# Two hybrid layers on one core: the merge and its gates get memory beside the attention

## The chip, the core and the metric

The kernel runs on one core of one Trainium2 chip. The metric is the device time of one execution in microseconds. The engines are TensorE (PE, with its weight loads as PEld), VectorE (DVE), ScalarE (ACT), GpSimd (POOL) and SyncE (SP), which here only issues transfers. All matrix products accumulate in PSUM; operands live in SBUF.

## What is computed

A model of two layers on 512 tokens of width 1024. Each layer is a feed-forward block, a mixer and a second feed-forward block. The mixer has three branches, which are gated and summed before one output product:

```python
def hybrid_mixer(...):
    proj = h @ w_in
    ret_p, dsa_p, rwkv_p, gate_p = split_cols(proj, GROUP_SIZES)
    y_ret = retention(...)          # ends: silu(g) * o
    y_dsa = sparse_attention(...)   # top-256 keys by an index score, then softmax
    y_rwkv = rwkv7_time_mix(...)    # a recurrence over tokens
    g_ret, g_dsa, g_rwkv = jnp.split(jax.nn.sigmoid(gate_p), N_BRANCH, axis=-1)
    merged = g_ret * (y_ret @ p_ret) + g_dsa * (y_dsa @ p_dsa) + g_rwkv * (y_rwkv @ p_rwkv)
    return merged @ w_out
```

All is float32. The kernel makes each large product from three products of split operands: a value is stored as a high part (`hi`, rounded) and the remainder (`lo`), and `hi*hi + hi*lo + lo*hi` is summed.

## The kernel before

Activations are held transposed, as 8 tiles of 128 x 512. `dense` (L116) makes one 128 x 512 output block: for each of its input blocks three matmuls (`mm3`, L105, whose lines are L109, L111 and L113). Weights come in pieces of 128 x 512 (`raw`, four buffers, L53), and each piece is split by `split` (L49 on ACT for the high part, L50 on DVE for the remainder) into `whi` and `wlo` (three buffers each). The output goes to one of four PSUM tiles `psd`.

The mixer runs two streams of work. The first is the recurrence, class `Rwkv`: four pairs of heads, one after another. For a pair, `next` prepares operands (`front2`, `mid`), `chain` (L505) goes through eight chunks of 64 tokens, and `post` (L545) normalises. A chunk of the chain is four small steps on PE (L512, L522, L532, L539) with a small DVE copy or update between each two, so that PE would wait at every step. These have the highest priority ("rec").

The second stream is `other` (L922), a Python generator: the index and the retention, the attention (`attend`, L785), 32 gate products (`gates`, L858) and the merge (`merge`, L874). `fill` (L73) takes a number of matmuls from it at each step of the recurrence, by the tables FZ to FF (L224 to L230), so that large products stand between the small steps. The attention's own work after its projection (L799 to L839) is written in one piece and placed by the scheduler, which follows priorities and its own estimate of when operands are ready. The final order on each engine is fixed when the program is built.

`gates` computes first, for each of 8 blocks, the gate of the retention output: it loads the block `yret[b]` from DRAM, multiplies it and stores it to `yg[b]`. Then it computes 24 gate factors, tanh values that it stores to `thd`. `merge` loads the gated outputs, splits them into `yh0`..`yh7` and `yl0`..`yl7`, and computes per branch (8, 4 and 4 input blocks) eight output blocks, with a `th` tile loaded for each; the sums are kept in tiles `m0`..`m7`. The third branch waits until the recurrence is done. It has 8 x 3 x (8 + 4 + 4) = 384 matmuls per layer. At the end the merged sums are split (`mh`, `ml`) and multiplied with `w_out` (192 matmuls, L958), and the residual `x` is loaded back (L955) and added.

Memory decides what may overlap. Pools are stacked from two sides of SBUF, and a tile in a new pool waits for the tiles that had its addresses before. `gp` lies where the retention's pool was. `mrg` is opened after the attention's pool `dsa` is closed, and lies on its addresses:

```python
            yield from ds.attend(a["wt"][l, 4])
            with right("gp") as gp:
                yield from gates(K, l, gp, a, yd[0], yg, thd)
        with right("mrg") as mp:
            yield from merge(K, l, mp, mh, a, (yg, yd[1], yd[2]), thd, rw)
```

Of the kernel before, what the change touches and what calls it, by code (L numbers as in the profile page):

```python
# [7 lines left out]
P = 128  # L8
F32 = mybir.dt.float32
F32R = mybir.dt.float32r  # L10
# [3 lines left out]
ALU = mybir.AluOpType  # L14
T = 512
# [6 lines left out]
class Core:  # L22
    def __init__(self, tc, ctx):
        self.tc, self.nc, self.ctx = tc, tc.nc, ctx
        self.n = 0
        self.work, self.urgent, self.between = iter(()), deque(), True
        self.early = deque()
        self.level = {"rec": 0, "split": 200000, "norm": 400000, "late": 800000}
        pool = lambda n, **kw: ctx.enter_context(tc.tile_pool(name=n, bufs=1, **kw))
        self.psp = pool("psp", space=bass.MemoryType.PSUM)  # L30
        self.cp = pool("cp")
        self.wp = pool("wp")
        self.xp = pool("xp")
        self.dp = pool("dp", space=bass.MemoryType.DRAM)
# [198 lines left out]
class Rwkv:  # L233


    def __init__(self, K, pool, par, w2a2, g2, cst, y_out):
        self.K, self.nc, self.tc, self.p = K, K.nc, K.tc, pool
        self.cst, self.y_out = cst, y_out
        self.gate, self.done = None, False
        nc = self.nc  # L240
        self.par = self.t("par", [P, NPAR])
        nc.sync.dma_start(self.par, par)

        raw = self.t("tha")
        nc.sync.dma_start(raw, w2a2)
        self.wa = self.stack(raw)
        self.g2 = self.t("g2")
        nc.sync.dma_start(self.g2, g2)
        self.bones = self.t("bones", [P, P], dt=F32R)
        nc.vector.tensor_copy(self.bones, cst["bones"])  # L250
        self.omm = self.t("omm", [P, 14])
# [64 lines left out]
    def pairs(self, blk):  # L316
        K = self.K
        K.run(self.lora(blk))
        K.run(self.front(0, blk))
        self.blk = blk  # L320
        K.fill(F0)
        nxt = self.next(0)
        for p in range(4):
            d = nxt
            K.fill(FM[p])
            with K.at("rec"):
                self.chain(d)
            K.fill()
            if p < 3:
                nxt = self.next(p + 1)  # L330
            with K.at("rec"):
                self.post(d)
        self.done = True
# [515 lines left out]
def gate(K, w, tl):  # L849

    ps = yield from K.dense(w, K.xg)
    g, th = tl("g", 2), tl("th", 2)
    K.nc.vector.tensor_tensor(out=g, in0=ps, in1=K.rb, op=ALU.mult)
    K.nc.scalar.activation(th, g, AF.Tanh, scale=0.5)
    return g, th


def gates(K, l, pool, a, yret, yg, thd):  # L858

    nc = K.nc  # L860
    tl = lambda tag, bufs=1, dt=F32: pool.tile([P, T], dt, tag=tag, name=K.nm(tag), bufs=bufs)
    for b in range(8):
        x = tl("y", 2)
        nc.sync.dma_start(x, yret[b])
        g, th = yield from gate(K, a["wf"][l, 14 + b], tl)
        nc.vector.scalar_tensor_tensor(out=g, in0=th, scalar=1.0, in1=g, op0=ALU.add, op1=ALU.mult)
        nc.vector.scalar_tensor_tensor(out=x, in0=g, scalar=0.5, in1=x, op0=ALU.mult, op1=ALU.mult)
        nc.sync.dma_start(yg[b], x)
    for j, d in enumerate(thd):
        _, th = yield from gate(K, a["wf"][l, 22 + j], tl)  # L870
        nc.sync.dma_start(d, th)


def merge(K, l, pool, mh, a, yd, thd, rw):  # L874

    nc = K.nc
    tl = lambda tag, bufs=1, dt=F32: pool.tile([P, T], dt, tag=tag, name=K.nm(tag), bufs=bufs)
    mg = []
    for br, (nb, o, pw) in enumerate(((8, 0, "pret"), (4, 0, "pdsa"), (4, 4, "prw"))):
        while br == 2 and not rw.done:  # L880
            yield "wait"
        y = []
        for b in range(nb):
            x = tl("y", 2)
            nc.sync.dma_start(x, yd[br][b])
            hi, lo = tl(f"yh{o + b}", dt=F32R), tl(f"yl{o + b}", dt=F32R)
            K.split(x, hi, lo)
            y.append((hi, lo))
        for j in range(KC):
            i = 8 * br + j  # L890
            if i < len(thd):
                th = tl("th", 2)
                nc.sync.dma_start(th, thd[i])
            else:
                _, th = yield from gate(K, a["wf"][l, 22 + i], tl)
            pp = yield from K.dense(a[pw][l, j], y)
            if br == 0:
                m = tl(f"m{j}")
                mg.append(m)
                nc.vector.scalar_tensor_tensor(out=m, in0=th, scalar=1.0, in1=pp, op0=ALU.add, op1=ALU.mult)  # L900
            else:
                nc.vector.scalar_tensor_tensor(out=th, in0=th, scalar=1.0, in1=pp, op0=ALU.add, op1=ALU.mult)
                nc.gpsimd.tensor_tensor(out=mg[j], in0=mg[j], in1=th, op=ALU.add)
            if br == 2:
                K.split(mg[j], *mh(j))


def mixer(K, l, a, c, xd, xnew, out_cb, done):
    nc, tc = K.nc, K.tc
    yd = [[K.dram([P, T], f"y{br}_{b}") for b in range(nb)] for br, nb in enumerate((8, 4, 4))]  # L910
    yg = [K.dram([P, T], f"yg_{b}") for b in range(8)]
    thd = [K.dram([P, T], f"th_{b}") for b in range(NTH)]
    right = lambda n: tc.tile_pool(name=K.nm(n), bufs=1, side="right", reuse_waits="tile")

    def y_dsa(qt, b, y):
        nc.sync.dma_start(yd[1][b][:, qt * P:qt * P + P], y)

    blk = lambda b: K.dense(a["wf"][l, b], K.xg)
    rp = tc.alloc_tile_pool(name=K.nm("rw"), bufs=1, reuse_waits="tile")
    rw = Rwkv(K, rp, a["rpar"][l], a["w2a2"][l], a["g2"][l], dict(c, idg=a["idg"]), lambda p, y: nc.sync.dma_start(yd[2][p], y))  # L920

    def other():  # L922
        with right("dsa") as dp:
            ds = Dsa(K, dp, c, y_dsa)
            with right("ret") as tp:
                rt = Ret(K, tp, dict(c, dmask=a["dmask"], qdec=a["qdec"]), lambda h, y: nc.sync.dma_start(yd[0][h], y))
                yield from ds.index(a["wd"][l])
                yield "index"
                for q in range(4):
                    yield from rt.quarter(q, a["wt"][l, q])  # L930
            yield from ds.attend(a["wt"][l, 4])
            with right("gp") as gp:
                yield from gates(K, l, gp, a, yd[0], yg, thd)
        with right("mrg") as mp:
            yield from merge(K, l, mp, mh, a, (yg, yd[1], yd[2]), thd, rw)

    hp = None
    mhl = []

    def mh(j):  # L940
        nonlocal hp
        if hp is None:
            rp.release()
            hp = tc.alloc_tile_pool(name=K.nm("mh"), bufs=1, reuse_waits="tile")
        mhl.append(tuple(hp.tile([P, T], F32R, tag=f"{n}{j}", name=K.nm(n)) for n in ("mh", "ml")))
        return mhl[-1]

    K.work = other()
    while next(K.work) != "index":
        pass  # L950
    rw.pairs(blk)
    K.run(K.work)
    x = xnew()
    for o in range(KC):
        nc.sync.dma_start(x[o], xd[o])  # L955
    with tc.tile_pool(name=K.nm("nrm"), bufs=1, reuse_waits="tile") as np_:
        for o in range(KC):
            pt = K.run(K.dense(a["wo"][l, o], mhl))  # L958
            nc.vector.scalar_tensor_tensor(out=x[o], in0=pt, scalar=0.5, in1=x[o], op0=ALU.mult, op1=ALU.add)
            out_cb(o, np_)  # L960
        done(np_)
    hp.release()


def hybrid(tc, a, out):
# [140 lines left out]
```

## Time and profile before

| | us |
|---|---|
| median of 3 runs | 3084.24 |
| lowest and highest | 3083.97, 3087.45 |
| the profiled execution | 3093.85 |
| its span, first to last instruction | 3092.0 |
| PE busy | 2989.0 |
| DVE busy | 1752.5 |
| ACT busy | 1077.6 |
| POOL busy | 713.5 |

The profile is one execution. Busy time of PE counts overlapping matmuls once; a 128 x 512 product is in the engine for about 0.39 us, and the next starts 0.23 us after it. The granted clock of TensorE has two levels, 2.4 GHz (1.00 in the views) and 1.2 GHz (0.50); over the whole span it is 0.972. Layer one's mixer lies at about 400 to 1180 us, layer two's at 1930 to 2715 us.

### The profile page before, as it was taken

The numbers are of one execution on the slowest core, as the hardware profiler recorded it, in microseconds if no ns is written. First come the engines' busy times: TensorE is split into PE (matmuls) and PEld (weight loads), VectorE is DVE, ScalarE is ACT, GpSimd is POOL, SyncE is SP. The second block draws the span as 40 slices with busy tenths as digits, with TensorE's granted clock in tenths as the row PEclk, the third lists the DMA queues.
The fourth block names the chain that finished last, engine by engine and source line by source line (L and its number), as shares of the span: only waits on it lengthen the run. The fifth ranks groups of instructions, "written<-read, shape, count | busy, mean of one in ns | idle before, by whom it ended". The sixth has DMA issues, their size and how long they took to land.

```text
span 3092.0 us, 40671 instructions
## 1 busy us (share of the span) xinstructions
PE 2989.0 (97%) x14336; PEld 2372.8 (77%) x14336; DVE 1752.5 (57%) x3641; ACT 1077.6 (35%) x1892; POOL 713.5 (23%) x1186
## 2 busy tenths in 40 slices
PE   9999999999999899999999999999999999999998
PEld 7888886677776678888888888766777767788886
DVE  5443386958585565444344433878585755644433
ACT  4333352233433233333333333423334433333322
POOL 2110024352324031111011101333424240311100
PEclk9999998999999799999999999989999988999999
DMA  4333332223323353233333334221333324533332
GB/s 135 99 96 106 114 93 60 69 81 120 110 91 106 111 187 96 96 97 96 95 97 97 96 109 117 81 67 56 101 112 100 101 88 145 169 95 96 97 94 89
DMA packets 203580, 314.08 MB, mean 102 GB/s; under 512 B 46320, under 2 KB 60400, under 8 KB 203376
## 3 DMA queue, kind: packets, MB, share of 16 engines
q1 hardware_dynamic: 203376, 311.49, 33.1%
q8 instruction: 112, 1.84, 0.2%
q14 instruction: 92, 0.75, 0.1%
HBM read 277.86 MB, written 33.55 MB: 101 GB/s over the span
## 4 chain that ended last, share of the span: by engine, by line
PE 80%; DVE 8%; DMA 5%; POOL 3%; issue 2%; ACT 1%; SPq 0%; DVEq 0%; POOLq 0%; ACTq 0%
PE psd L109 23%; PE psd L113 23%; PE psd L111 23%; DMA N<-dn 2%; DVE wlo L50 2%; POOL E L474 1%; PE psf L96 1%; DMA th<-th 1%; POOL cum L476 1%; PE psr L512 1%; PE psf L660 1%; PE psf L662 1%; PE psr L429 1%; PE psf L719 1%; DMA y<-y 1%
## 5 line engine op out<-in xcount | busy, mean ns | idle before, releaser
L49 ACT ACTIVATE whi<-raw 128x512 fp32r<-128x512 f32 (+2 forms) x920 | 570.9, 621 | 1227.3 <-PE psd L111 932.7
L50 DVE TENSOR_TENSOR wlo<-raw,whi 128x512 fp32r<-128x512 f32 (+2 forms) x920 | 661.6, 720 | 547.8 <-ACT whi L49 533.3
L109 PE MATMUL psd<-xh,whi 128*128 128x512 f32 x2144 | 854.1, 398 | 1.5 <-DVE g L203 1.5
L111 PE MATMUL psd<-xl,whi 128*128 128x512 f32 x2144 | 848.9, 396 | 2.2 <-DVE xl L161 2.2
L113 PE MATMUL psd<-xh,wlo 128*128 128x512 f32 x2144 | 847.4, 395 | 0.1
L109 PEld LDWEIGHTS psd<-xh,whi 128*128 128x128 f32 x2144 | 405.7, 189 | 87.4 <-DVE g L203 1.7
L111 PEld LDWEIGHTS psd<-xl,whi 128*128 128x128 f32 x2144 | 405.8, 189 | 87.3 <-DVE xl L161 4.3
L113 PEld LDWEIGHTS psd<-xh,wlo 128*128 128x128 f32 x2144 | 405.5, 189 | 85.4 <-issue 1.8
L207 POOL TENSOR_TENSOR u<-s,u 128x512 f32<-128x512 f32 x88 | 140.9, 1602 | 841.3 <-DVE u L206 745.1
L109 PE MATMUL psd<-ah,whi 128*128 128x512 f32 x704 | 277.4, 394 | 0.0
L113 PE MATMUL psd<-ah,wlo 128*128 128x512 f32 x704 | 276.0, 392 | 0.0
L111 PE MATMUL psd<-al,whi 128*128 128x512 f32 x704 | 273.2, 388 | 0.0
L172 POOL TENSOR_TENSOR sq<-sq,sq 128x512 f32<-128x512 f32 x42 | 56.1, 1336 | 467.7 <-ACT sq L170 467.7
L111 PE MATMUL psd<-wlo,xh 128*128 128x512 f32 (+1 forms) x384 | 153.6, 400 | 3.9 <-DVE wlo L50 3.9
L113 PEld LDWEIGHTS psd<-ah,wlo 128*128 128x128 f32 x704 | 132.1, 188 | 30.9
L111 PEld LDWEIGHTS psd<-al,whi 128*128 128x128 f32 x704 | 132.2, 188 | 29.6
L113 PE MATMUL psd<-whi,xl 128*128 128x512 f32 (+1 forms) x384 | 153.9, 402 | 0.0
L109 PEld LDWEIGHTS psd<-ah,whi 128*128 128x128 f32 x704 | 132.3, 188 | 26.3
L50 DVE TENSOR_TENSOR al<-u,ah 128x512 fp32r<-128x512 f32 x88 | 61.8, 702 | 153.6 <-ACT ah L49 153.5
L109 PE MATMUL psd<-whi,xh 128*128 128x512 f32 (+1 forms) x384 | 144.0, 401 | 0.0
L206 DVE TENSOR_TENSOR u<-psd,rb 128x512 f32<-128x512 f32 x88 | 60.8, 691 | 127.6 <-PE psd L113 127.6
L818 POOL TENSOR_SCALAR L<-L,mx 128x128 f32<-128x128 f32 (+3 forms) x64 | 72.4, 1132 | 196.6 <-DVE mx L817 146.1
(262 smaller groups left out, 3909.5 us busy)
## 6 DMA issues: line engine op xcount, KB each, us to landing
raw<-in_wf_dram SPq DMA_DIRECT2D x184, 256.0 KB
raw<-in_ffa_in_dram SPq DMA_DIRECT2D x176, 256.0 KB
raw<-in_ffb_in_dram SPq DMA_DIRECT2D x176, 256.0 KB
th<-th SPq DMA_DIRECT2D x96, 256.0 KB
raw<-in_ffa_out_dram SPq DMA_DIRECT2D x80, 256.0 KB
raw<-in_wt_dram SPq DMA_DIRECT2D x80, 256.0 KB
raw<-in_ffb_out_dram SPq DMA_DIRECT2D x80, 256.0 KB
x<-x SPq DMA_DIRECT2D x32, 256.0 KB
```

The lines of the kernel that those rows point to most:

```text
L49: self.nc.scalar.activation(hi, x, AF.Copy)
L50: self.nc.vector.tensor_tensor(out=lo, in0=x, in1=hi.bitcast(F32), op=ALU.subtract)
L96: return self.nc.tensor.transpose(out, x, self.ident)
L109: nc.tensor.matmul(out, ah, bh, start=start, stop=False)
L111: nc.tensor.matmul(out, ah, bl, start=False, stop=False)
L113: nc.tensor.matmul(out, al, bh, start=False, stop=stop)
L172: nc.gpsimd.tensor_tensor(out=sq, in0=sq, in1=self.ssq[0], op=ALU.add)
L206: nc.vector.tensor_tensor(out=u, in0=pu, in1=self.rb, op=ALU.mult)
L207: nc.gpsimd.tensor_tensor(out=u, in0=s, in1=u, op=ALU.mult)
L429: zl = nc.tensor.matmul(z[:, i * P:(i + 1) * P], bk[s, ck, :], st[h][s, ck, :], start=True, stop=True)
L474: nc.gpsimd.tensor_tensor(out=tv, in0=X[:, 0:n, u:u + 1].to_broadcast([P, n, w]), in1=N[:, u:u + 1, u + 1:].to_broadcast([P, n, w]), op=AL ...
L818: nc.gpsimd.tensor_scalar(out=x, in0=x, scalar1=mx[:, 3:4], scalar2=None, op0=ALU.mult)
```

## The change

The gates and the merge share one pool `mrg`, opened on the left beside the recurrence's pool, so that it lies on none of the attention's addresses. Its size is made to fit in three ways. The gated retention output is no longer stored and reloaded: `gates` splits it at once into `yh`, `yl` and hands these to `merge`. The merged sums lie in eight tiles of the recurrence (MTAGS), which are free after the last pair has been prepared; `merge` waits for the flag `late` before it takes them. The reload tile `y` has one buffer instead of two. The area at the bottom of SBUF that is reserved for descriptors shrinks from 16 KB to 1 KB per partition. The residual `x` and the high parts of the merged sums get tiles where the attention was; the low parts take the tiles of `yh` and `yl`.

```diff
@@ class Rwkv, pairs
             if p < 3:
                 nxt = self.next(p + 1)
+                self.late = p == 2
@@ gates
     for b in range(8):
-        x = tl("y", 2)
+        x = tl("y")
         nc.sync.dma_start(x, yret[b])
         g, th = yield from gate(K, a["wf"][l, 14 + b], tl)
...
-        nc.sync.dma_start(yg[b], x)
+        ys.append((tl(f"yh{b}", dt=F32R), tl(f"yl{b}", dt=F32R)))
+        K.split(x, *ys[b])
@@ merge
+MTAGS = ("r", T), ("k", T), ("v", T), ("tha", T), ("kh", T), ("cum", 520), ("E", 520), ("P", T + 1)
...
-    mg = []
+    while not rw.late:
+        yield "wait"
+    mg = [rw.t(tag, [P, n], 2 if tag == "P" else 1)[:, :T] for tag, n in MTAGS]
...
-        y = []
-        for b in range(nb):
-            x = tl("y", 2)
+        y = [] if br else yr
+        for b in range(nb if br else 0):
+            x = tl("y")
             nc.sync.dma_start(x, yd[br][b])
@@ mixer, other
-            yield from ds.attend(a["wt"][l, 4])
-            with right("gp") as gp:
-                yield from gates(K, l, gp, a, yd[0], yg, thd)
-        with right("mrg") as mp:
-            yield from merge(K, l, mp, mh, a, (yg, yd[1], yd[2]), thd, rw)
+        yield from ds.attend(a["wt"][l, 4])
+        dp.release()
+        box["x"] = xnew()
+        box["p"] = tc.alloc_tile_pool(name=K.nm("mh"), bufs=1, side="right", reuse_waits="tile")
+        mp = box["m"] = tc.alloc_tile_pool(name=K.nm("mrg"), bufs=1, reuse_waits="tile")
+        ys = yield from gates(K, l, mp, a, yd[0], thd)
+        yield from merge(K, l, mp, mh, a, ys, yd, thd, rw)
@@ kernel
-    nc = _bacc.Bacc("TRN2", target_bir_lowering=False, num_devices=1)
+    nc = _bacc.Bacc("TRN2", target_bir_lowering=False, num_devices=1, dynamic_dma_scratch_size=1024)
```

What moves is best seen in the built order. On PE, layer one, at the start of the last chain (L522 is a chain step, L831 and L832 are value products of the attention, L718 and L719 its logits), there stands before, after the last gate product:

```order
L113 MATMUL psd_9232<-xh_2985,wlo_9275 128x512
L522 MATMUL psr_9446<-cx_9454,mt_9251 64x64 x2
L831 MATMUL psf_6482<-X_6501,v_3127 128x256
L532 MATMUL psr_9446<-uv_2125_9456,bkt_8844 64x64
...
L718 MATMUL psf_6516<-kh_3322,qs_6404 128x512
L719 MATMUL psf_6516<-kl_3323,qs_6404 128x512
L512 MATMUL psr_9496<-sv_2001_8857,stk_1972_8724 128x64
```

and after the change, at the same place (lines of the recurrence and the attention are one higher; `yh` and `yl` are the split retention output):

```order
L113 MATMUL psd_9263<-xh_2985,wlo_9306 128x512
L109 MATMUL psd_9405<-yh_1586_6893,whi_9408 128x512
L111 MATMUL psd_9405<-yl_1587_6894,whi_9408 128x512
L113 MATMUL psd_9405<-yh_1586_6893,wlo_9409 128x512
...
L523 MATMUL psr_9420<-cx_9428,mt_9282 64x64 x2
L109 MATMUL psd_9405<-yh_1682_7315,whi_9438 128x512
L111 MATMUL psd_9405<-yl_1683_7316,whi_9438 128x512
L113 MATMUL psd_9405<-yh_1682_7315,wlo_9439 128x512
...
L832 MATMUL psf_6474<-X_6493,v_3119 128x256
L533 MATMUL psr_9420<-uv_2123_9430,bkt_8875 64x64
```

Merge products now stand between the chain's steps; before, the first of them stands behind the whole chain. On SP, layer one, at the end of the attention, there stand before the reloads of the gated output (`yg`) and of the attention's output, with the transfers of the weights behind them:

```order
L916 DMA y_3_661_3057<-kil_6613 128x128
L885 DMA y_9318<-yg_666_3062 128x512
L893 DMA th_9366<-th_674_3070 128x512
L885 DMA y_9330<-yg_668_3064 128x512
L54 DMA raw_9680<-in_pret_dram 128x512
L885 DMA y_9972<-y_0_658_3054 128x512
L885 DMA y_9978<-y_1_659_3055 128x512
```

and after the change, behind the same store of the attention's last output (now L919):

```order
L919 DMA y_3_661_3057<-kil_6605 128x128
L956 DMA x_6614<-x_1_73 128x512
L54 DMA raw_9977<-in_pdsa_dram 128x512
L956 DMA x_6618<-x_5_77 128x512
L54 DMA raw_10000<-in_pdsa_dram 128x512
L901 DMA th_9827<-th_672_3068 128x512
L895 DMA y_9956<-y_1_659_3055 128x512
L54 DMA raw_10092<-in_pdsa_dram 128x512
L895 DMA y_9962<-y_2_660_3056 128x512
```

The reloads of `yg` are gone, the eight loads of `x` have come forward from the output stage to here, and the reloads of the attention's output stand one by one between weights.

## Rows read from the trace of the kernel before

**Rows 1.** The page, part 1: busy time of each engine, share of span.

```profile
PE 2989.0 (97%) x14336; PEld 2372.8 (77%) x14336; DVE 1752.5 (57%) x3641; ACT 1077.6 (35%) x1892; POOL 713.5 (23%) x1186
```

**Rows 2.** Windows: bounds, length, busy us (instructions) per engine, clock, DMA share, GB/s.

```profile
300.00:350.00 50.00, 50.00 (x220) 41.04 (x219) 18.41 (x28) 16.63 (x28) 5.38 (x4) 1.00 0.40 116
...
992.90:1042.50 49.60, 38.51 (x180) 26.66 (x179) 31.89 (x113) 11.17 (x22) 9.01 (x16) 0.55 0.14 47
1042.50:1135.35 92.85, 89.06 (x382) 69.62 (x382) 55.80 (x76) 28.50 (x47) 22.92 (x15) 1.00 0.57 178
2528.70:2576.00 47.30, 38.39 (x182) 26.40 (x181) 31.77 (x111) 11.16 (x22) 9.04 (x16) 0.57 0.15 49
2576.00:2668.05 92.05, 88.90 (x380) 70.78 (x378) 56.25 (x77) 28.38 (x47) 23.35 (x15) 0.98 0.58 179
```

**Rows 3.** PE timeline: start, us, line, product, and idle before with releaser.

```profile
992.66 0.47 PE L113 MATMUL psd<-xh,wlo 128*128 128x512 f32 x1
...
1036.69 1.22 PE L109 MATMUL psd<-yh,whi 128*128 128x512 f32 x2 [4.03 <-ACT yh L49]
...
1135.35 0.40 PE L109 MATMUL psd<-mh,whi 128*128 128x512 f32 x1
...
2668.05 0.40 PE L109 MATMUL psd<-mh,whi 128*128 128x512 f32 x1
```

**Rows 4.** Six chunks of the third chain: its window; PE's groups, busy us, mean ns.

```profile
851.64:880.63 28.99, 28.07 (x180) 19.81 (x177) 21.95 (x82) 8.55 (x19) 7.80 (x16) 1.00 0.21 67
...
L109 PE MATMUL psd<-xh,whi 128*128 128x512 f32 x18 | 8.8, 491 | 0.0
...
L512 PE MATMUL psr<-sv,stk 128*128 128x64 f32 x22 | 4.4, 280 | 0.4 <-DVE sv L535 0.4
L96 PE MATMUL psf<-ident,L 128*128 128x128 f32 x12 | 2.3, 272 | 0.0
...
L522 PE MATMUL psr<-cx,mt 64*64 64x64 f32 x24 | 2.0, 242 | 0.5 <-DVE cx L515 0.5
...
L719 PE MATMUL psf<-kl,qs 64*128 64x384 f32 x4 | 1.7, 436 | 0.0
L832 PE MATMUL psf<-X,v 128*128 128x256 f32 x6 | 1.7, 298 | 0.0
...
L718 PE MATMUL psf<-kh,qs 128*128 128x384 f32 x4 | 1.4, 353 | 0.0
```

**Rows 5.** PE's groups, 992.9 to 1032.2 us (two rows), 1042.5 to 1054 (two).

```profile
L96 PE MATMUL psf<-ident,L 128*128 128x128 f32 x17 | 5.0, 418 | 0.0
...
L832 PE MATMUL psf<-X,v 128*128 128x256 f32 x10 | 4.6, 465 | 0.9 <-DVE X L50 0.9
...
L572 PE MATMUL psr<-sg,g 128*128 128x512 f32 x2 | 1.1, 630 | 0.0
L96 PE MATMUL psr<-ident,Y 128*64 128x128 f32 x8 | 1.0, 272 | 0.0
```

**Rows 6.** ACT and SP timelines: splits of reloaded outputs, and issues of their loads.

```profile
1040.69 1.30 ACT L49 ACTIVATE yh<-y 128x512 fp32r<-128x512 f32 x2 [3.39 <-DMA y<-yg]
...
1037.39 6.21 SPq L885 DMA_DIRECT2D y<-yg  x4
```

**Rows 7.** Window of the first gates; the page's group of splits; DVE and POOL timelines.

```profile
690.00:780.00 90.00, 86.53 (x504) 65.12 (x503) 76.32 (x221) 34.03 (x75) 22.20 (x36) 1.00 0.39 122
...
L50 DVE TENSOR_TENSOR wlo<-raw,whi 128x512 fp32r<-128x512 f32 (+2 forms) x920 | 661.6, 720 | 547.8 <-ACT whi L49 533.3
...
984.20 1.28 DVE L50 TENSOR_TENSOR wlo<-raw,whi 128x512 fp32r<-128x512 f32 x1
...
983.64 1.29 POOL L569 TENSOR_TENSOR bc<-bc,bv 128x512 f32<-128x512 f32 x1 [0.76 <-DVE bc L567]
```

**Rows 8.** SP timeline: the loads of the residual; the window in which they land.

```profile
1143.71 3.84 SPq L955 DMA_DIRECT2D x<-x  x8
...
1150.00:1154.00 4.00, 4.00 (x20) 3.26 (x19) 1.43 (x3) 1.24 (x2) 1.34 (x1) 1.00 1.04 387
```

More of the change, by code (lines that the diff above doesn't have):

```diff
@@ L238, in __init__ @@
         self.cst, self.y_out = cst, y_out
-        self.gate, self.done = None, False
+        self.gate, self.done, self.late = None, False, False
         nc = self.nc
@@ L855, in gate, with gates @@
     return g, th
-def gates(K, l, pool, a, yret, yg, thd):
+def gates(K, l, pool, a, yret, thd):
     nc = K.nc
     tl = lambda tag, bufs=1, dt=F32: pool.tile([P, T], dt, tag=tag, name=K.nm(tag), bufs=bufs)
+    ys = []
     for b in range(8):
-        x = tl("y", 2)
+        x = tl("y")
         nc.sync.dma_start(x, yret[b])
@@ L871, in gates, with merge @@
         nc.sync.dma_start(d, th)
-def merge(K, l, pool, mh, a, yd, thd, rw):
+    return ys
+MTAGS = ("r", T), ("k", T), ("v", T), ("tha", T), ("kh", T), ("cum", 520), ("E", 520), ("P", T + 1)
+def merge(K, l, pool, mh, a, yr, yd, thd, rw):
     nc = K.nc
     tl = lambda tag, bufs=1, dt=F32: pool.tile([P, T], dt, tag=tag, name=K.nm(tag), bufs=bufs)
-    mg = []
+    while not rw.late:
+        yield "wait"
+    mg = [rw.t(tag, [P, n], 2 if tag == "P" else 1)[:, :T] for tag, n in MTAGS]
     for br, (nb, o, pw) in enumerate(((8, 0, "pret"), (4, 0, "pdsa"), (4, 4, "prw"))):
@@ L889, in merge @@
         for j in range(KC):
[L890 to L895, printed above, removed]
+            th, m = tl("th", 2), mg[j]
+            nc.sync.dma_start(th, thd[8 * br + j])
             pp = yield from K.dense(a[pw][l, j], y)
             if br == 0:
-                m = tl(f"m{j}")
-                mg.append(m)
                 nc.vector.scalar_tensor_tensor(out=m, in0=th, scalar=1.0, in1=pp, op0=ALU.add, op1=ALU.mult)
@@ L902, in merge @@
                 nc.vector.scalar_tensor_tensor(out=th, in0=th, scalar=1.0, in1=pp, op0=ALU.add, op1=ALU.mult)
-                nc.gpsimd.tensor_tensor(out=mg[j], in0=mg[j], in1=th, op=ALU.add)
+                nc.gpsimd.tensor_tensor(out=m, in0=m, in1=th, op=ALU.add)
             if br == 2:
-                K.split(mg[j], *mh(j))
+                K.split(m, *mh(j))
 def mixer(K, l, a, c, xd, xnew, out_cb, done):
@@ L910, in mixer @@
     yd = [[K.dram([P, T], f"y{br}_{b}") for b in range(nb)] for br, nb in enumerate((8, 4, 4))]
-    yg = [K.dram([P, T], f"yg_{b}") for b in range(8)]
     thd = [K.dram([P, T], f"th_{b}") for b in range(NTH)]
@@ L920, in mixer @@
     rw = Rwkv(K, rp, a["rpar"][l], a["w2a2"][l], a["g2"][l], dict(c, idg=a["idg"]), lambda p, y: nc.sync.dma_start(yd[2][p], y))
+    box, mhl = {}, []
     def other():
[L923 to L930, printed above, removed]
-            yield from ds.attend(a["wt"][l, 4])
-            with right("gp") as gp:
-                yield from gates(K, l, gp, a, yd[0], yg, thd)
-        with right("mrg") as mp:
-            yield from merge(K, l, mp, mh, a, (yg, yd[1], yd[2]), thd, rw)
-    hp = None
-    mhl = []
-    def mh(j):
[L941 to L946, printed above, removed]
+        dp = tc.alloc_tile_pool(name=K.nm("dsa"), bufs=1, side="right", reuse_waits="tile")
+        ds = Dsa(K, dp, c, y_dsa)
+        with right("ret") as tp:
+            rt = Ret(K, tp, dict(c, dmask=a["dmask"], qdec=a["qdec"]), lambda h, y: nc.sync.dma_start(yd[0][h], y))
+            yield from ds.index(a["wd"][l])
+            yield "index"
+            for q in range(4):
+                yield from rt.quarter(q, a["wt"][l, q])
+        yield from ds.attend(a["wt"][l, 4])
[5 more added lines that the diff above has]
+        yield from merge(K, l, mp, mh, a, ys, yd, thd, rw)
+    def mh(j):
+        lo = box["m"].tile([P, T], F32R, tag=f"y{'hl'[j // 4]}{j % 4}", name=K.nm("ml"), bufs=1)
+        mhl.append((box["p"].tile([P, T], F32R, tag=f"mh{j}", name=K.nm("mh")), lo))
+        return mhl[j]
     K.work = other()
@@ L952, in mixer @@
     K.run(K.work)
-    x = xnew()
+    x = box["x"]
     for o in range(KC):
@@ L961, in mixer @@
         done(np_)
-    hp.release()
+    box["m"].release()
+    box["p"].release()
+    rp.release()
 def hybrid(tc, a, out):
```

## The prediction

> **What bounds the kernel now.** First the busy table, then equal windows, then PE's timeline at the places where the windows differ. The reader should see that PE is busy for 97% of the span [rows 1], so only stretches in which PE's work is slow or thin can give time back. In an ordinary feed-forward stretch PE starts 220 dense products in 50 us, one per 0.227 us, with the clock granted in full [rows 2]; nothing can be won there, and the order of the instructions there is the same in both programs.
>
> The weak places are one per layer, at the recurrence's last chain. In the first layer the last gate product starts at 992.66, and the first merge product runs at 1036.69, after 4.03 us of waiting for a split of a reloaded retention output [rows 3]. In between PE has only the chain and the attention. From 992.9 to 1042.5 it is busy 38.5 of 49.6 us, at a granted clock of 0.55; from 2528.7 to 2576 it is 38.4 of 47.3 us at 0.57 [rows 2]. A mean of 0.55 is nearly all time at the lower level, 1.2 GHz. The merge then runs alone at the full clock until 1135.35 and 2668.05 [rows 2, 3].
>
> **What it should cost instead.** The span from the last gate product to the first output product is 1135.35 - 992.9 = 142.4 us and 2668.05 - 2528.7 = 139.3 us [rows 2, 3]. I price the work in it at the full clock.
>
> Merge: 384 products x 0.227 = 87.2 us.
>
> Chain and attention at full clock: I take six chunks of the chain before it, where 54 dense products (three groups of 18) are mixed in and the clock is 1.00 [rows 4]. Of 28.99 us, 54 x 0.227 = 12.3 are dense and 28.99 - 28.07 = 0.9 idle, so 15.8 remain. The chain's four groups there show 4.4 + 3 x 2.0 = 10.4 us of overlapping busy time, the attention's 2.3 + 2 x 1.7 + 1.7 + 1.4 = 8.8 [rows 4]. Splitting 15.8 in that ratio gives 8.6 us for the chain, 1.43 per chunk, and 7.2 for the attention. The last chain has eight chunks less one opening pair that has already run: 11.0 us. Its attention has 17 transposes for 12, 20 value products for 12, and eight logit products that are 512 wide (the order shows them) instead of 384 [rows 4, 5]: 2.3 x 17/12 + 3.4 x 20/12 + 3.1 x 4/3 = 13.1, times 15.8/19.2, is 10.8 us. The last post pass adds 1.0 + 1.1 us of busy time [rows 5], 1.7 by the same ratio.
>
> The work is therefore 87.2 + 11.0 + 10.8 + 1.7 = 110.7 us per layer. The kernel loses 142.4 - 110.7 = 31.7 us in the first layer and 28.6 in the second, 60.3 together, to the low clock and to idle time. That is all the change can get.
>
> Busy time alone would say less: 11.1 us of idle PE in the first layer's stretch. By the busy share of weight loads, 26.7 of 49.6 us (0.54) against 41.0 of 50 (0.82) in the dense stretch [rows 2], there are 17 us. Slow weight loads count as busy too, so I keep the count of products.
>
> **The change, part by part.**
>
> Memory. The order shows 138 of the 384 merge products standing among the last chain's chunks, five between one chain step and the next; before, none stands there. They need 138 x 0.227 = 31.4 us, so the stretch becomes 31.4 + 21.8 = 53.2 us and PE is 59% dense in it, against 42% in the six chunks that ran at 1.00 [rows 4]. I therefore give it the full clock. What can hold it is VectorE: it is busy 31.9 us today in that stretch [rows 2], and 138/24 = 5.75 accumulations bring two weight splits (0.72) and one sum (about the same) each, 12.4 us. That is at most 44 of 53 us, 83%; the six chunks had 76% and 0.9 us of PE idle [rows 4], so I charge 1.5 us per layer, between 0 and 5.
>
> Gated output split on chip. 8 stores and 8 loads of 256 KB per layer disappear, and with them the waits on those loads at the merge's start [rows 6]. The eight split pairs move into the first chain and the next pair's preparation. VectorE is busy 76.3 of 90 us there and PE 86.5 [rows 7]; 8 x 0.72 = 5.8 us make that 82. I charge 1.5 us per layer, between -1 and 5.8 (every split on PE's path). One weight split there took 1.28 us, against a mean of 0.72 [rows 7].
>
> Single buffer for loads. The reload tile has one buffer instead of two. Today a load issued at 1037.39 lets the next split start at 1040.69, 3.3 us later, and a split pair is 0.65 + 0.72 us [rows 6, 7], so a single buffer turns over in about 4.7 us. At the change from retention to attention products the first y is already there and its split waits, as before, for the last retention accumulation to have read the tile. From then the fourth y is ready after 1.4 + 3 x 4.7 = 15.5 us. PE has 21 products, three rounds of nine, and the post pass to do, 4.8 + 6.1 + 1.7 = 12.6 us. The stall is 2.9; I charge 3, between 0 and 10.
>
> What stays. The merge alone has 92.85 - 89.06 = 3.8 us of idle today, and 3.2 in the second layer [rows 2], mostly late weight splits. I keep 4, between 3 and 5.
>
> Moved loads. The eight loads of the residual x are issued at the end of the attention instead of in the output stage; there they took a burst of 387 GB/s [rows 8]. Their 2.1 MB need 5.4 us in front of the attention products' weights. Cover: some 12 us of retention products that are still to run; without it, up to 5.4 us per layer (inside the 10 above).
>
> Sums in the recurrence's tiles, later release of the pools, and the smaller descriptor scratch move no instruction on PE's path; every DMA is issued by SP. The fill cannot run dry: the order of the products from the second chain to the last gate product is unchanged. I take zero, +-2 us.
>
> **The sum.** Losses after: 1.5 + 1.5 + 3 + 4 = 10 us per layer. The saving is 60.3 - 20 = 40 us. The profiled execution (3093.85 us, span 3092.0) would become 3054; it stands 9.6 us above the median of the runs. I apply the saving to the median: 3084.24 - 40 = **3044**. With the bounds, losses per layer run from 2 to 26, that is 3028 to 3076.
>
> **Rivals.**
>
> The crowded changeover: x loads, gate factors, weights and y loads, 16 x 256 KB = 4.2 MB, meet in 12 us, 10.8 at the burst rate [rows 8]. For it: today the merge alone draws 178 GB/s [rows 2], half as much. Against: four weight buffers and three split buffers run ahead. Price 7 us per layer more: 3058.
>
> Better than forecast: splits hide, the changeover is covered, losses are 3 per layer: 3030.
>
> Less room than counted: if the weight loads' share is the better measure, 17 us per layer come back and the time is 3084 - 34 = 3050. The Trainium skill, "Perfetto Trace Analysis" (Identifying the Most-Contended Engine), prefers that measure: matmul busy share is no good sign of headroom there, and the busy share of weight loads is. The trace agrees that the two differ (11 and 17 us), and no run here shows yet which is nearer.
>
> Splits held up by GpSimd: if each of the eight moved splits lasts 1.28 us like the one in rows 7, VectorE has 8 x 0.56 = 4.5 us per layer more, and if PE feels it all the time is 3053. The mean of 0.72 over all such instructions speaks against it. The Trainium skill, "SBUF — State Buffer" (Who interferes with whom), has a rule for it: a VectorE instruction with two SBUF inputs and a GpSimd instruction that reads SBUF exclude each other, whichever issues first. It speaks against putting these splits beside the attention's GpSimd work; the one long split, during a GpSimd product [rows 7], agrees with it.
>
> The other side, the single buffer as the new bound: seven y loads pass one after another through SP's queue, behind weights and x. After the last y, 69 products (15.7 us) remain, so the merge's end is 1.4 + 7p + 15.7 us after the retention products, for a turnover p. At p = 4.7 that is 50 us, under PE's own 53. The whole gain is gone when the end is 20 us later, at p = 8.0; at twice today's turnover, 9.4 us, it is 83, and the time 3044 + 2 x 30 = 3104. Nothing in rows 6 is that slow, and weight loads already pass between.
>
> The clock stays low in the mixed stretch: at half the clock 138 products cost 31 us more and the chain and attention some 22 more, as they do today, 3044 + 106 = 3150. It decides above 20 us per layer. Rows 4 speak against it.
>
> Nothing moves: the merge products wait for something other than memory, 3084. Their operands (gated outputs) exist long before, and weights are loaded ahead.
>
> **How the numbers follow.** The predicted time is the forecast's; forecast 0.52, crowded changeover 0.17, better 0.10, less room 0.07, held-up splits 0.05, single buffer 0.04, low clock 0.02, nothing 0.03. Range 3028 to 3062: it leaves out the last three and the far part of the second and third. A measurement of this kernel can tell about 0.2% (6 us) from no change. Faster 0.91, same 0.03, slower 0.06.
>
> **What would show it.** In the stretch of the last chain the granted clock should read 0.95 or more, PE over 95% busy, and the 4 us wait for a reloaded y should be gone. From the last gate product to the first output product it should take about 119 us in each layer. A wait of PE for a split of y in front of the attention products above 5 us would speak for the crowded changeover; the same before the recurrence's products, for the single buffer. More idle of PE in the first chain than today would make the 1.5 us wrong.

## The result, and the profile after

The changed kernel took 3057.64 us (3051.45 to 3062.89) beside 3085.84 us for the kernel before, a ratio of 0.9908, 95% interval 0.9887 to 0.9928: 28 us less, where 40 were forecast. A second measurement of it (a_again, below) gave 0.9897. The profiled execution took 3062.89 us, its span 3061.1, 30.9 us less than the span of before. First the busy table after, which answers to [rows 1].

```profile
PE 2965.2 (97%) x14336; PEld 2352.3 (77%) x14336; DVE 1748.0 (57%) x3641; ACT 1076.7 (35%) x1892; POOL 714.8 (23%) x1186
```

PE has 24 us less of busy time for the same number of products: what was slow has become faster. The windows show where. These are the last chain (from the last gate product on) and the rest of the merge, for both layers; columns as in [rows 2], to which they answer.

```profile
1003.30:1056.00 52.70, 52.70 (x305) 38.58 (x303) 35.31 (x108) 14.76 (x28) 9.61 (x16) 1.00 0.38 118
1056.00:1122.27 66.27, 62.57 (x257) 47.66 (x257) 46.96 (x72) 20.73 (x34) 21.87 (x15) 0.97 0.59 184
2518.90:2571.00 52.10, 52.10 (x300) 38.31 (x298) 35.21 (x108) 14.76 (x28) 9.61 (x16) 1.00 0.34 112
2571.00:2636.09 65.09, 60.89 (x263) 47.13 (x262) 44.17 (x72) 19.71 (x33) 20.63 (x15) 1.00 0.60 193
```

The last chain now runs without one idle microsecond and at the full clock, where it had 0.55 and 0.57 and 38.5 of 49.6 us busy. PE's timeline gives the ends of the stretch and the largest wait in it, as [rows 3] did for before.

```profile
1003.08 0.48 PE L113 MATMUL psd<-xh,wlo 128*128 128x512 f32 x1
1003.39 0.39 PE L109 MATMUL psd<-yh,whi 128*128 128x512 f32 x1
...
1080.24 0.97 PE L109 MATMUL psd<-yh,whi 128*128 128x512 f32 x3 [1.88 <-ACT yh L49]
...
1122.27 0.39 PE L109 MATMUL psd<-mh,whi 128*128 128x512 f32 x1
...
2518.67 0.48 PE L113 MATMUL psd<-xh,wlo 128*128 128x512 f32 x1
...
2636.09 0.40 PE L109 MATMUL psd<-mh,whi 128*128 128x512 f32 x1
```

From start to start it is 1122.27 - 1003.08 = 119.2 us and 2636.09 - 2518.67 = 117.4 us, against 142.7 (1135.35 - 992.66) and 139.6 us before. That is 23.5 + 22.2 = 45.7 us won. But the last gate product of the first layer itself starts at 1003.08 instead of 992.66. As the mark for the recurrence's second chain (the one in which the gates begin, called the first chain in the prediction) I take the last step of its first chunk. For the first layer that is the first line below before and the second after; the third line is the last gate product of the second layer before.

```profile
703.92 0.33 PE L539 MATMUL psr<-uv,zb 64*64 64x64 f32 x4
...
702.62 0.33 PE L540 MATMUL psr<-uv,zb 64*64 64x64 f32 x4
...
2528.49 0.47 PE L113 MATMUL psd<-xh,wlo 128*128 128x512 f32 x1
```

From this mark to the last gate product it was 288.7 us before and is 300.5 now; in the second layer 292.5 and 299.0. That is 11.7 + 6.5 = 18.2 us lost. In a second profile of the changed kernel (a_again) it is 9.1 + 6.0. The rest of the program is 3.4 us shorter: 45.7 - 18.2 + 3.4 = 30.9.

The loss is largest in front of the third pair. PE waits there for `bc`, a copy on VectorE at the end of a row of small dependent steps, and then for `cum`; first before, then after.

```profile
764.23 0.66 PE L96 MATMUL psr<-ident,bc 128*128 128x128 f32 x4 [3.06 <-DVE bc L384]
801.66 0.19 PE L478 MATMUL psr<-ident,cum 128*1 128x1 f32 x2 [3.03 <-POOL cum L476]
```

```profile
769.28 1.11 PE L96 MATMUL psr<-ident,bc 128*128 128x128 f32 x4 [6.54 <-DVE bc L385]
806.24 0.19 PE L479 MATMUL psr<-ident,cum 128*1 128x1 f32 x2 [4.36 <-POOL cum L477]
```

Two windows of 40 us at that place, of before and then of after:

```profile
740.00:780.00 40.00, 36.94 (x179) 28.83 (x178) 38.56 (x89) 15.88 (x31) 11.05 (x10) 1.00 0.39 118
780.00:820.00 40.00, 36.97 (x175) 28.59 (x174) 18.73 (x40) 16.37 (x33) 20.39 (x57) 0.96 0.34 105
```

```profile
740.00:780.00 40.00, 33.14 (x147) 25.67 (x146) 37.80 (x84) 17.45 (x32) 11.27 (x12) 0.91 0.24 77
780.00:820.00 40.00, 35.64 (x175) 27.96 (x174) 18.63 (x43) 14.85 (x31) 15.35 (x44) 0.91 0.37 107
```

VectorE was busy for 38.56 of 40 us there already before the change, 96%; in the next 40 us for 18.73. Four of the eight splits stand in the full window (from 750.17 to 771.88 us), the other four between 703 and 737. The row of steps from `s` to `bc` on VectorE, before and then after, shows what they do there:

```profile
753.88 0.16 DVE L381 TENSOR_SCALAR s<-psr 128x8 f32<-128x8 f32 x1
...
763.76 0.42 DVE L384 COPY bc<-kkr 128x512 f32<-128x512 f32 x1
```

```profile
755.18 0.15 DVE L382 TENSOR_SCALAR s<-psr 128x8 f32<-128x8 f32 x1
...
768.81 0.42 DVE L385 COPY bc<-kkr 128x512 f32<-128x512 f32 x1
```

The row takes 13.6 us instead of 9.9, and PE waits 3.5 us longer for its end. Between its ends stand five more instructions of 128 x 512 than before, two of the splits, one weight remainder and two of the gates, of some 0.69 us each.

### The profile page after: what moved, and what is told of

It is laid out like the page before. It is cut to its first block, busy times and chain, and to the rows that moved or that the text cites. A ratio compares the mean times of both kernels' runs of the same rounds, so it can differ in the third digit from the quotient of the medians.

```text
span 3061.1 us, 40579 instructions
## 1 busy us (share of the span) xinstructions
PE 2965.2 (97%) x14336; PEld 2352.3 (77%) x14336; DVE 1748.0 (57%) x3641; ACT 1076.7 (35%) x1892; POOL 714.8 (23%) x1186
## 4 chain that ended last, share of the span: by engine, by line
PE 79%; DVE 9%; DMA 5%; POOL 3%; issue 2%; ACT 1%; SPq 0%; DVEq 0%; POOLq 0%; ACTq 0%
PE psd L109 23%; PE psd L113 23%; PE psd L111 23%; DMA N<-dn 3%; DVE wlo L50 2%; POOL E L475 1%; DMA y<-y 1%; POOL cum L477 1%; PE psf L96 1%; PE psf L661 1%; PE psr L513 1%; DMA th<-th 1%; PE psf L663 1%; PE psf L720 1%; PE psr L430 1%
## 5 line engine op out<-in xcount | busy, mean ns | idle before, releaser
L50 DVE TENSOR_TENSOR wlo<-raw,whi 128x512 fp32r<-128x512 f32 (+2 forms) x920 | 649.1, 707 | 530.0 <-ACT whi L49 514.8
```

The source lines that it names most:

```text
L50: self.nc.vector.tensor_tensor(out=lo, in0=x, in1=hi.bitcast(F32), op=ALU.subtract)
```

## The experiments

Ratios are to the kernel before, which ran beside each of these kernels on the same chip. The changed kernel has 0.9908 (0.9887 to 0.9928).

**The splits alone, on the kernel before (b_split).**

```diff
         nc.sync.dma_start(yg[b], x)
+        K.split(x, tl(f"qh{b % 2}", dt=F32R), tl(f"ql{b % 2}", dt=F32R))
```

> The kernel before, with one part of the change alone: each of the eight gated retention outputs of a layer is also split on chip, into two pairs of tiles that nothing reads (so the splits are extra work and the output is unchanged); the round trip through DRAM and both y buffers stay. Theory A (VectorE's queue): the eight extra VectorE instructions of 0.69 us stand in front of the recurrence's copies bc and cum, PE waits longer there and its clock falls; this costs what the changed kernel lost between the first chain and the second, some 11 us in layer one and 6 in layer two, 3085 + 17 = 3102, with a bc wait of about 6.5 us instead of 3.06. Theory B (the single y buffer makes VectorE wait for a load, and all behind it): two buffers are kept here, so nothing is lost, 3085 +- 4, bc wait about 3 us.

Measured: 3108.12 us, ratio 1.0049 (1.0033 to 1.0064), 15 us more. PE's largest wait at the place, and the same 40 us:

```profile
771.78 0.47 PE L96 MATMUL psf<-ident,L 128*128 128x128 f32 x1 [7.80 <-POOL L L818]
...
740.00:780.00 40.00, 31.87 (x144) 24.86 (x145) 36.94 (x84) 17.18 (x33) 12.84 (x14) 0.87 0.32 98
```

The wait is 7.80 instead of 3.06 us. (In front of the `bc` transposes now stands one of the attention; its releaser, a GpSimd step, had itself waited for VectorE, and `bc` was copied at 770.61.) By the marks above the kernel loses 8.9 us in the first layer and 6.0 in the second. So eight split pairs per layer in this place cost 15 us with two y buffers and with nothing else changed. Theory A holds, and theory B doesn't explain this.

**Two y buffers in the changed kernel (a_y2).**

```diff
-        x = tl("y")
+        x = tl("y", 2)
...
-dynamic_dma_scratch_size=1024
+dynamic_dma_scratch_size=128
```

> The changed kernel with two y buffers instead of one (the descriptor area is 128 bytes per partition instead of 1 KB, which makes just enough room that no tile of the merge lies on the attention's addresses). Theory A (VectorE's queue): the splits stay where they are, the bc wait stays at about 6.5 us, and only the changeover between retention and attention products (1.9 us of waiting per layer) can get better: 3050 to 3058. Theory B (single buffer): the loss between first and second chain goes, bc wait about 3 us, 3057 - 17 = 3040.

Measured: 3060.77 us, 0.9896 (0.9878 to 0.9914), not to be told from the changed kernel. The wait in front of the third pair is 7.81 us. The single buffer is not what the changed kernel lost by. (The smaller descriptor area was not run by itself.)

**Retention gates spread among the gate factors (a_spread).**

```diff
-    for b in range(8):
-        x = tl("y")
...
     for j, d in enumerate(thd):
         _, th = yield from gate(K, a["wf"][l, 22 + j], tl)
         nc.sync.dma_start(d, th)
+        b = (j - 1) // 2
+        if j < 1 or (j - 1) % 2 or b > 7:
+            continue
+        x = tl("y")
...
```

> The changed kernel with the 32 gate products of a layer in another order: the eight retention gates, each with its product and its split, come one after every two of the gate factors instead of all eight first. The same instructions, spread over the second and third chain as well. Theory A (VectorE's queue in the first chain): the bc wait in front of the second pair falls to 3 us or below and the loss of 17 us goes: 3040, or up to 3048 if other chains pay part of it. Rival (the loss comes with the lower clock at that place whatever VectorE does, or the load just moves on): 3053 to 3060.

Measured: 3058.8 us, 0.9896 (0.9876 to 0.9916). The `bc` wait in front of the third pair (the expectation calls it the second) is gone: there is no wait over 0.75 us until that for `cum`. The second chain and what follows it, up to the third chain, takes 151.7 instead of 158.2 us. But the next waits grew: 5.48 us for `cum` in place of 4.36, 4.79 in front of the fourth pair in place of 2.72. From second chain to last gate product it is 297.9 us against 300.5, and 296.0 against 299.0. Expected were up to 17 us. The load moved on with the splits, as the rival said; each retention gate now stands at some other place on the recurrence's way.

**The low parts by GpSimd (a_pool).**

```diff
-        K.split(x, *ys[b])
+        nc.scalar.activation(hi, x, AF.Copy)
+        nc.gpsimd.tensor_tensor(out=lo, in0=x, in1=hi.bitcast(F32), op=ALU.subtract)
```

> The changed kernel with the low parts of the eight gated retention outputs computed by GpSimd instead of VectorE; place and order are the same otherwise. Theory A (the eight VectorE instructions cost PE time in the first chain): the bc wait falls from 6.5 us to about 3 and the time by about 15 us against the changed kernel, a ratio to the kernel before near 0.986. Rival C (the tail is latency of the whole gate, not VectorE's time): the same within 4 us, ratio 0.990. Rival D (GpSimd beside VectorE slows both): slower than the changed kernel, ratio above 0.992.

Measured: 3068.23 us, 0.9928 (0.9916 to 0.994); nearest to rival D, though the lower end of the interval lies under its 0.992. The `bc` wait fell to 3.68 us, but other waits came (1.26 us for `qs`, 3.04 for a GpSimd step, 4.63 for `cum`). VectorE's groups from 690 to 790 us, first of the changed kernel, then of this one (line, shapes, count, busy us and mean ns of one):

```profile
L50 DVE TENSOR_TENSOR wlo<-raw,whi 128x512 fp32r<-128x512 f32 x20 | 14.1, 707 | 0.2
L868 DVE SCALAR_TENSOR_TENSOR g<-th,g 128x512 f32<-128x512 f32 x8 | 5.4, 680 | 0.0
L532 DVE TENSOR_SCALAR cb<-sv,gch 64x64 f32<-64x64 f32 x14 | 4.0, 285 | 0.2
```

```profile
L50 DVE TENSOR_TENSOR wlo<-raw,whi 128x512 fp32r<-128x512 f32 x21 | 18.1, 862 | 1.5 <-ACT whi L49 1.3
L868 DVE SCALAR_TENSOR_TENSOR g<-th,g 128x512 f32<-128x512 f32 x8 | 6.5, 816 | 0.0
L532 DVE TENSOR_SCALAR cb<-sv,gch 64x64 f32<-64x64 f32 x14 | 6.4, 458 | 0.2
```

The three groups take some 7 us more (one of the 21 splits belongs to a later product) while VectorE is spared 5.5 us. None of them was edited. Four of the instructions that grew ran during one of the eight: three remainders, at 703.03, 725.78 and 777.22 us (1.65, 1.50 and 1.34 us), and a `cb` pair at 714.56 (1.58). Beyond their usual length they hold 3.5 of the 7 us. Three others, at 747.99, 753.22 and 754.81, ran beside GpSimd instructions that the changed kernel has too. The Trainium skill, "SBUF — State Buffer" (Who interferes with whom), has a VectorE instruction with two SBUF inputs, such as the first two, contend with a GpSimd instruction that reads SBUF, and names tensor_scalar, the third, among those that can take the shared port under conditions; the groups agree with it. "Perfetto Trace Analysis" of the Trainium skill (Optimizing Scalar/DVE Operations) draws the consequence, that "offloading operations between those two might not help". Here it did not help: by the ratios it cost 6 us against the first measurement of the changed kernel (0.9908, the intervals overlap) and 10 against the second (0.9897, they do not).

**Without the split in the gates (a_yg2, a_yg).** Stored, reloaded and split at the merge, as before the change; all else as changed, with two y buffers (and a descriptor area of 128 bytes) in a_yg2, and with the single one in a_yg.

```diff
-        ys.append((tl(f"yh{b}", dt=F32R), tl(f"yl{b}", dt=F32R)))
-        K.split(x, *ys[b])
+        nc.sync.dma_start(yg[b], x)
...
-        y = [] if br else yr
-        for b in range(nb if br else 0):
+        y = []
+        for b in range(nb):
```

> The changed kernel without the split in the gates: the gated retention output is stored, reloaded and split at the merge as before, with two y buffers; the merge keeps its own memory. Theory A: the first chain is as before (bc wait 3 us), which gives back 15 to 18 us; against that the eight loads and splits stand at the start of the last chain, where VectorE has room (83% at most by the count of the prediction): ratio to the kernel before 0.985 to 0.988. Rival (the splits cost the same wherever they stand, as the spread order hints, which gave 4 us and not 17): ratio 0.989 to 0.992.

> The changed kernel without the split in the gates (stored, reloaded and split at the merge, as before) but with its single y buffer. Theory: the split is what cost, so most of the gain of a_yg2 stays: ratio 0.986 to 0.988. Rival (a single buffer cannot feed eight reloads at the start of the merge: 8 turns of some 4.7 us are 37 us, in which 12 + 24 products are due): PE waits for yh at the start of the last chain and the ratio is 0.990 or above.

Measured: with two buffers 3047.57 us, 0.9863 (0.985 to 0.9877); with one 3063.89 us, 0.9903 (0.9888 to 0.9918). The first has the ratio that theory A expected, and the `bc` wait is 3.06 us again:

```profile
763.78 0.66 PE L96 MATMUL psr<-ident,bc 128*128 128x128 f32 x4 [3.06 <-DVE bc L385]
```

From the mark in the second chain to the last gate product it takes 4.1 and 1.5 us more than the kernel before, where the changed kernel takes 11.7 and 6.5 more, so most of the loss came back and not all of it. The loads and splits did not go to the start of the last chain, as I had written. The splits stand behind `bc`, from 769.66 to 793 us, five of the eight in the emptier window from 780 on. VectorE's group of these splits from 760 to 830 us, with two buffers and then with one:

```profile
L50 DVE TENSOR_TENSOR yl<-y,yh 128x512 fp32r<-128x512 f32 x8 | 5.5, 688 | 1.3 <-ACT yh L49 1.2
```

```profile
L50 DVE TENSOR_TENSOR yl<-y,yh 128x512 fp32r<-128x512 f32 x8 | 5.7, 713 | 9.1 <-ACT yh L49 9.0
```

With one buffer VectorE itself stands idle for 9.1 us in front of the eight splits. The single buffer costs something after all where eight reloads pass through it: 12 us between the two ratios, the size that the rival gave, though not at its place. Hardly any of it is lost beside this idle time. From the second chain to the third, by the same mark, the two kernels take 152.1 and 152.7 us (152.2 and 153.4 in the second layer); from there to the first output product it is 256.9 us with two buffers and 264.6 with one (256.1 and 263.5). What holds the second kernel up there is open.

**The merge held behind the chain (a_hold, a_hold2).** First by its flag alone, then by this flag and an order on PE (every merge product is placed after the chain's last matmul).

```diff
-    while not rw.late:
+    while not rw.done:
```

> The changed kernel with the merge held back until the recurrence is done, that is with the flag of the third branch in place of the one for the last pair; memory, the on-chip split, the moved loads and all else as changed. If the 138 merge products between the last chain's steps are the whole gain, the time from last gate product to first output product goes back from 119.0 and 117.1 us to about 140 (a bit less: the reloaded y is no longer waited for, 4.0 and 1.5 us), and the run takes 3057 + 40 = 3097, above the kernel before, since the loss in the first chain stays; the granted clock in the last chain is 0.55 again. Rival (part of the gain is the layout, or the reload of the gated output that is gone): 3057 to 3080.

```diff
+            if d["p"] == 3 and ck == 7:
+                K.hold = last
...
+            with ExitStack() as es:
+                if self.hold:
+                    es.enter_context(self.tc.issue_after(self.hold.ins))
                 nc.tensor.matmul(out, x, y, start=s, stop=e)
```

> The changed kernel with every merge product placed behind the last step of the recurrence's last chain on PE (in the run named a_hold the scheduler had moved them forward again, so that nothing was held back). Memory, splits and loads as changed. If the 138 products between the chain's steps are the gain, the stretch from last gate product to first output product is some 138 us in both layers again (142.4 and 139.3 before, less the wait for the reloaded y, 4.0 and 1.5 us), the granted clock of the last chain 0.55, and the time 19 + 21 = 40 us above the changed kernel: ratio to the kernel before 1.003. Rival (a good part of the gain is the reload that is gone and the loads moved forward): ratio 0.993 to 0.998.

The first gave 3095.46 us, 1.0011 (1.0002 to 1.002), but it is not the test that I meant: the scheduler moved merge products between the chain's steps all the same, and in another order. Its windows show something else: nearly all merge products are spent early, and at the chain's end nothing is left to cover it.

```profile
1090.00:1105.00 15.00, 11.64 (x55) 8.62 (x54) 9.34 (x20) 2.42 (x4) 5.57 (x4) 1.00 0.53 157
1105.00:1120.00 15.00, 5.28 (x13) 2.90 (x14) 5.88 (x17) 0.63 (x1) 1.26 (x1) 0.54 0.10 36
```

The second is the test: 3101.54 us, 1.0036 (1.0024 to 1.0048), expected 1.003. The stretch from last gate product to first output product is 138.1 and 137.1 us. Its last chain and merge:

```profile
1007.60:1049.00 41.40, 34.49 (x168) 23.44 (x168) 26.68 (x95) 8.02 (x17) 9.04 (x16) 0.54 0.14 42
1049.00:1145.60 96.60, 93.71 (x394) 73.09 (x394) 56.96 (x86) 27.68 (x45) 21.72 (x14) 0.99 0.55 172
```

The clock is at 0.54 again, and the whole kernel is slower than before the change. Between 1.0036 and 0.9908 lie 0.0128 of 3090 us: 40 us hang on the place of 138 products (with the weight splits that go with them), and without that the other edits cost 11 us.

**The loads of x (a_again, a_yg2x, a_x).** Put back to the output stage, in the kernel without the split (two buffers, a_yg2x) and in the changed kernel (a_x); the changed kernel itself ran once more beside the first (a_again).

```diff
     for o in range(KC):
+        nc.gpsimd.tensor_copy(x[o][:, :1], mhl[4][0].bitcast(F32)[:, :1])
         nc.sync.dma_start(x[o], xd[o])
```

> The changed kernel itself, unchanged, beside the two runs below on one chip, so that their ratios can be set against it directly. Expected: the ratio of its first measurement, 0.9908 within 0.002.

> The changed kernel without the split in the gates and with two y buffers (as a_yg2, which had 0.9863), and with the eight loads of the residual put back to the output stage: each waits for a one-column GpSimd copy out of the fifth merged sum, so that no x load stands in front of the attention products' weights. If the moved x loads hold up those weights (PE waited 1.80 us there for a weight's high part), 2 to 4 us less for both layers, ratio 0.985; if the loads were covered, as the prediction had it, the same, 0.9863; if they now collide with the output product's weights, slower, 0.988.

> The changed kernel with one part undone: the eight loads of the residual are back in the output stage, each behind a one-column GpSimd copy out of the fifth merged sum; the on-chip split in the gates and the single y buffer stay. In the run a_yg2x the same edit gave 0.9839 against 0.9863 without it, 7 us, of which the profiles showed 3.8 in the output stage (44.9 and 45.0 us for its products instead of 47.0 and 46.7). If that holds here: 4 to 7 us less than the changed kernel, ratio 0.988 to 0.989, output stages of 45 us. If it was scatter between chips or calls: the ratio of the changed kernel, 0.990 to 0.991.

Measured: the changed kernel again 3060.61 us, 0.9897 (0.988 to 0.9913); without the split and with late x loads 3042.27 us, 0.9839 (0.9824 to 0.9853), the best of all; the changed kernel with late x loads 3063.0 us, 0.9901 (0.9884 to 0.9919), no change, and its output stages take 46.2 and 46.6 us, not 45. So the moved loads cost the changed kernel nothing that these runs can tell. Whether they cost the better version the 7 us between 0.9863 and 0.9839 is not settled: the intervals touch, and the two ran on different chips. That the better version beats the change by 18 us is direct: the two ran side by side on one chip.

**Several edits together (a_best1):** two buffers, spread gates, low parts by GpSimd.

> Three edits together on the changed kernel: two y buffers, retention gates spread one after every two gate factors, low parts by GpSimd. Theory A: the spread order took 3.7 us, two buffers 2.6 us by the profile of the last stretch, GpSimd up to 15; together no more than the 18 us lost plus 3: ratio to the kernel before 0.984 to 0.987. If GpSimd does not help: 0.989.

Measured: 3052.63 us, 0.9877 (0.9865 to 0.989), between what the two forecasts said. Here GpSimd's splits are spread out, and the `bc` wait is gone, but `cum` still makes PE wait 5.45 and 4.23 us. Taking the split out of the gates (a_yg2, on the same chip) took 5 us less, but the intervals overlap.

## Why the prediction was right, and where it was wrong

**The gain: right in its mechanism.** The prediction wrote 110.7 us of work and 1.5 + 3 + 4 of losses for the stretch, 119.2; it is 119.2 and 117.4. The full clock in the mixed stretch, worked out from the six chunks of the chain before [rows 4], is there: 1.00 where 0.95 was asked for. VectorE is busy 35.3 of 52.7 us, not up to 44, and PE does not wait for it, so the 1.5 us charged there are 0. PE's idle time in the rest of the merge is 66.27 - 62.57 = 3.7 us and 4.2, where 3 + 4 were charged for the changeover and the late weight splits. That the sum agrees so closely is in part luck: PE is busy in this rest for 62.57 and 60.89 us, where 246 x 0.227 + 1.7 = 57.5 us of work were priced. Too little work and too much loss were written, and they nearly cancel. The wait of 4.03 us for a reloaded y at the start of the merge is gone. The run with the merge held back shows the cause: the same kernel with those 138 products behind the chain is 40 us slower.

**The failed step: "The eight split pairs move into the first chain and the next pair's preparation … I charge 1.5 us per layer, between -1 and 5.8."** It measured 11.7 and 6.5 us, above its upper bound in both layers (9.1 and 6.0 in the second profile). Two things were wrong in it. First, I read VectorE's load from one window of 90 us [rows 7], 76.3 busy, and saw room for 5.8. In its last 40 us, 740 to 780, VectorE was at 96%, and PE already waited 3.06 us for it; nearly all the room was elsewhere. Second, the upper bound took the instructions' own time for the worst that PE can feel. PE's idle time between the second and the third chain grew by more than that: 14.8 us now (158.20 - 143.39) against 6.6 (147.50 - 140.87), and 14.2 against 5.9 in the second layer, 8.2 and 8.3 us more for 5.5 us of VectorE work.

```profile
703.90:851.40 147.50, 140.87 (x771) 106.76 (x770) 105.21 (x282) 57.78 (x121) 47.88 (x108) 0.99 0.36 110
2236.00:2386.80 150.80, 144.90 (x771) 109.84 (x770) 104.79 (x281) 57.80 (x121) 48.43 (x108) 0.95 0.34 107
```

```profile
702.60:860.80 158.20, 143.39 (x769) 108.19 (x768) 110.06 (x289) 61.34 (x128) 48.28 (x107) 0.96 0.31 92
2219.70:2376.50 156.80, 142.56 (x771) 107.67 (x770) 109.64 (x289) 61.52 (x128) 48.04 (x108) 0.96 0.30 93
```

The first fence is before, the second after. They also tell the two layers apart. In the first the clock fell with the idle time, 0.99 to 0.96, and the busy time rose by 2.5 us; in the second it was low already before, 0.95, and the busy time fell by 2.3. That is the difference between 10.7 and 6.0 us in this interval. b_split shows 15 us of such a loss without any other part of the change, so the term is that of the splits. Of the 8.2 us in the first layer, 3.5 are the longer wait for `bc`, at the end of the row that five more instructions stretch, 1.3 the longer wait for `cum`, and 1.6 two waits for `cx` in the second chain (0.64 and 0.98 us) where none was over 0.6 before. Why the sum is more than the splits' own time is shown for `bc` only, where instructions of the gates have moved into the row together with the splits.

**The rivals.** The crowded changeover has the time that came out, 3058, but not the mechanism: PE waits 1.88 us there, and neither two buffers nor late x loads changed the changed kernel. The range reached up to 3062 because it took this rival in. That it so covers a time that came from another term, one that broke its own bound, is luck. Less room than counted: the share of weight loads gave 17 us per layer, and 23.5 and 22.2 came back, so the share was too low. The count of products gave 31.7 and 28.6, less 8.5 of losses in the stretch 23.2 and 20.1, which is near. The Trainium skill, "Perfetto Trace Analysis" (Identifying the Most-Contended Engine), names the busy share of weight loads as a measure of headroom, and beside it the work done against the peak, which is the kind of measure that the count is. Here the two differ: a weight load of the chain (of `psr<-sv,stk`) lasted 296 ns on average in the last chain before, at the low clock, and 188 ns in it after, and the longer load is busy time too. Held-up splits: the eight last 691 ns on average in that stretch, not 1.28 us; the place was right, the reason not. The single buffer as the bound did not come about in the changed kernel; in a_yg, where eight more reloads use it, a single buffer cost some 12 us.

**What the change is made of.** Merge products between the last chain's steps are worth 40 us by a_hold2. The on-chip split takes back 10 to 14 of them: 0.9863 without it and with a second buffer (a_yg2), against 0.9896 with both (a_y2) and 0.9908. With a descriptor area of 128 bytes the second buffer fits, so neither the split nor the single buffer is needed for the merge to have its place.

## What to carry to other kernels

A stretch whose large products run out at a low clock can be brought near to its work at the full clock, and that can be counted from a neighbouring stretch: here to within 2 us per layer, with two errors that nearly cancelled. Memory that forbids the overlap is worth freeing. Before work is moved onto an engine, look at its busy share in windows as short as the dependent row that it may hold up: 85% over 90 us was 96% over the 40 that mattered, with an idle PE behind it. A DMA round trip that nobody waits for can be worth keeping: here the same splits cost less where the reload let them stand behind the row that PE waits for.

## What the runs showed of the hardware

With eight more GpSimd instructions of 1365 ns, VectorE instructions that were not edited took some 7 us more, above the 8 x 0.69 us that VectorE was spared; about half of it fell on four that ran during one of the eight (a_pool). A single buffer let VectorE idle for 9.1 us in front of eight splits (a_yg). Waits of PE of 6.5 to 7.8 us go with a granted clock of 0.91 and 0.87 over the 40 us around them, where 3.06 us before left 1.00 in the first layer, but a wait of the same length went with 0.91 in the second.
